# Three edits to a two-layer kernel on one core: how attention's probabilities are turned, and where four of the modulation's vectors are made

## The chip, the cores and the metric

The kernel runs on one core of a Trainium2 chip, as one launch. The metric is device time in microseconds (us), the median of several runs. A core has five engines with queues of their own: TensorE (PE in the profile; its weight loads are PEld), VectorE (DVE), ScalarE (ACT), GpSimd (POOL) and SyncE (SP), which here only issues DMAs; 16 DMA engines move the data between HBM and the core's memory SBUF. TensorE writes to PSUM.

## The reference, cut to what matters

Two layers of a diffusion transformer over 1024 rows of 1024 columns (x) and 256 rows of context (ctx). Each layer makes six vectors of 1024 from the conditioning c, the modulation:

```
m = silu(cond) @ w + b
sh1, sc1, gt1, sh2, sc2, gt2 = split(m, 6)
hx = rmsnorm(x, g) * (1 + sc1) + sh1
x = x + gt1 * mixer(hx)
x = x + gt2 * ec_moe(modulate(x, norm_ffn_g[layer], sh2, sc2))
```

So vectors 3 and 4 of a layer (sh2, sc2) are the shift and scale ahead of its experts, and vectors 2 and 5 are gates. Layer 0's mixer is a chunked mLSTM (4 heads) beside window attention (8 heads of 64, two key heads, blocks of 128 queries that see up to three blocks of keys and the 256 of the context, softmax with a sink); layer 1's is a gated MLP. `ec_moe` lets each of 16 experts take its 128 best rows by a router's softmax (top k over rows), runs silu(x Wg) * (x Wu) Wd on them with three 1024x1024 weights, and adds the result back to those rows.

## The kernel before, in words

All arithmetic is float32. A float32 product that must be exact is split: each operand into a high part (rounded to the fp32r type) and a low part, and three fp32r matmuls (high-high, low-high, high-low) stand for one. ScalarE makes the high part, VectorE the low one by a subtraction (`split`, L70 and L71). A scheduler puts the instructions of each engine into a fixed order, by the order in which the program writes them and by when it expects their inputs; tiles come from pools with a number of slots, and an instruction waits until its slot is free.

Stages, with their time in the profile:

- *Start* (0 to about 92): `start` loads ctx and x (pool "xp", ten slots of 128x1024, tag "xt"), makes layer 0's vectors 0 and 1 for x and ctx (`start_mod`), normalizes the rows and turns them. `heads_context` makes keys and values of the mLSTM's context: for each of four heads two projections, with a convolution between; between the projections it takes steps from a generator (`more`) that turns x into columns.
- *Attention and projections* (92 to 600): `layer0_a`. `attention` goes over four pairs of heads and eight blocks of 128 queries each. For a block: scores S in PSUM, their maximum (VectorE), the exponential P with its sum (ScalarE), the reciprocal of the sum. Then P (128 queries x 512 or 640 keys) is turned to keys x queries, block by block of 128x128, and split (PH, PL) for the product with the values. Before, the turn is a matmul of the block with a diagonal matrix `dg` that holds the reciprocals, so one matmul turns and divides (L480, L492). Between these parts, `fill(n)` takes steps of other work out of a generator: the projections of the next heads (L298, three 128x512 matmuls for each of eight column blocks), and now and then one step of the modulation, 9 of them for 28 steps.
- The modulation's other ten vectors come from `mod_part` (L660): for each of eight row blocks of w_mod a 128x1024 tile (0.5 MB, issued on POOL, two slots) and four matmuls that use a quarter of TensorE's columns each (L670, two passes, so eight instructions), then the bias (VectorE), and either a row written out (gates) or two transposes and a copy into `modc`.
- *mLSTM and output projection* (600 to 820), `layer0_b`; near its end each finished block of rows goes through the router (`route_tile`).
- *Routing* (820 to 862): `route` finds each expert's 128th largest score by sorting on VectorE; TensorE does little. `lists` makes row lists; `fetch` gathers an expert's rows by an indirect DMA on POOL.
- *Experts* (862 to 1430): `experts`, for each expert gate, up and down product (L1134). Weights come as 1 MB tiles (256x1024) into a ring of slots with the tag "mraw" (`moe_tile`, `moe_raw`): two slots in "gx" and eight that `layer0_b` opens near 746, five more after it: 15. Loads go on SP's queue in order, each waiting for its slot. Those whose number lies in `HELD` = (11, 14) are issued on POOL behind expert 0's row gather instead (`self.fetched`), so that they don't stand before it.
- Layer 1's gated MLP (to about 2050), its routing and experts, and the final norm, to the end. They have their own ring (`mraws` is emptied first).

Of the kernel before, what the change touches and what calls it, by code (L numbers as in the profile page):

```python
# [18 lines left out]
D = 1024  # L19
N = 1024  # L20
NT = 8
KD = 8
# [16 lines left out]
class Kernel:  # L39
# [142 lines left out]
    def start(self, rings):  # L182
        nc, I = self.nc, self.I
        with ExitStack() as late:
# [32 lines left out]
            self.heads_context(late, pt, Ws, rows())  # L217

    def heads_context(self, s, pt, Ws, more):
# [225 lines left out]
    def attention(self, hp, c, Q, fill):  # L445
# [6 lines left out]
        for n in range(NT):  # L452
# [17 lines left out]
            for i in range(2):  # L470
# [16 lines left out]
            for i in range(2):  # L487
                if i:
                    fill(self.FILLS[1])
                P, dg = Ps[i]  # L490
# [60 lines left out]
    def layer0_a(self, rings):  # L551
        nc, I = self.nc, self.I
        with ExitStack() as s:
# [60 lines left out]
            mods = itertools.chain(*(self.mod_part(lm, pa, pt, i // 6, i % 6) for i in range(2, 12)))  # L614
# [4 lines left out]
            def fill(n):  # L619

                for _ in itertools.islice(work, n):
                    i = next(steps)
                    if 9 * (i + 1) // 28 > 9 * i // 28:
                        next(mods, None)
# [35 lines left out]
    def mod_part(self, pool, pa, pt, layer, w):  # L660


        nc, I = self.nc, self.I
        acc = pa.tile([128, 512], F32, tag="acc", name="acc")[:, 0:256]
        for k in range(KD):
            wm = pool.tile([128, D], F32, tag="wm", name="wm")
            nc.gpsimd.dma_start(out=wm, in_=I["w_mod"][layer, k * 128:(k + 1) * 128, D * w:D * (w + 1)])  # L667
            lhs = self.silw[:, k].rearrange("p a s -> p (a s)")
            for j in range(4):
                nc.tensor.matmul(acc[32 * j:32 * j + 32, :], lhs, wm[:, 256 * j:256 * (j + 1)], start=(k == 0), stop=(k == KD - 1))  # L670
            yield
        rows = pool.tile([128, 256], F32, tag="mrows", name="mrows", bufs=1)
        bias = pool.tile([128, 256], F32, tag="mbias", name="mbias", bufs=1)
        b = I["b_mod"]
        nc.gpsimd.dma_start(out=bias, in_=bass.AP(tensor=b.tensor, offset=b.offset + 6 * D * layer + D * w, ap=[[256, 4], [0, 32], [1, 256]]))
# [4 lines left out]
        else:  # L680
            tr = pt.tile([128, 512], F32, tag="tr", name="tr")
            for t in range(2):
                nc.tensor.transpose(tr[:, t * 128:(t + 1) * 128], rows[:, t * 128:(t + 1) * 128], self.ident)
            nc.vector.tensor_copy(self.modc[:, layer, 8 * w:8 * w + 8].rearrange("p (j t) -> p j t", t=2),
                                  tr[:, 0:256].rearrange("p (t j r) -> p j t r", t=2, j=4)[:, :, :, 0])
        yield

# [125 lines left out]
    def layer0_b(self, l0):  # L813
# [8 lines left out]
        with ExitStack() as s:  # L822
# [43 lines left out]
            self.moe_open(self.m0, 0, 8)  # L866
            lp = self.pool(s, "lp2")
# [94 lines left out]
    def route(self, p, pp, layer):  # L962
# [10 lines left out]
        nc.tensor.transpose(tr[:, 0:128], lg.rearrange("p t e -> p (t e)"), self.ident)  # L973
# [123 lines left out]
    def moe_raw(self, name, layer, e, kp):  # L1097
        held = self.HELD[0] <= self.mrawi < self.HELD[1]
# [9 lines left out]
    HELD = (11, 14)  # L1108
# [454 lines left out]
    def run(self):  # L1563
        nc = self.nc
        with ExitStack() as es:
# [53 lines left out]
            with ExitStack() as r:  # L1619
                rw = self.pool(r, "rw0")  # L1620
                pp = self.pool(r, "rpp0", bufs=3, space=PSUM)
                self.route(rw, pp, 0)
# [78 lines left out]
```

## Time and profile before

| | |
|---|---|
| runs before | 2724.99, 2725.24, 2725.42 us; median 2725.24 |
| profiled execution | 2720.4 us; span of its instructions 2718.6 us |
| TensorE busy | 2529.9 us, 93% |
| VectorE busy | 1879.9 us, 69% |
| ScalarE busy | 1511.4 us, 56% |
| GpSimd busy | 626.0 us, 23% |
| chain that ended last, by engine | TensorE 80%, VectorE 8%, DMA 4%, issue 4%, ScalarE 3%, GpSimd 1% |
| moved by DMA | 644 MB, 237 GB/s over the span |

How to read it: the busy share is a mean over stages of different kinds, so what an edit is worth is read from its own stage. Matmuls overlap: a row's duration is longer than the distance to the next one's start. The chain of waits follows the work back from the last instruction; "issue" is time in which nothing that the profile shows was waited for. PEclk is TensorE's granted clock, 1.00 being 2.4 GHz and 0.50 being 1.2 GHz. A DMA share of 1.0 means that all 16 DMA engines moved packets all the time.

### The profile page before, as it was taken

The numbers are of one execution on the slowest core, as the hardware profiler recorded it, in microseconds if no ns is written. First come the engines' busy times: TensorE is split into PE (matmuls) and PEld (weight loads), VectorE is DVE, ScalarE is ACT, GpSimd is POOL, SyncE is SP. The second block draws the span as 40 slices with busy tenths as digits, with TensorE's granted clock in tenths as the row PEclk, the third lists the DMA queues.
The fourth block names the chain that finished last, engine by engine and source line by source line (L and its number), as shares of the span: only waits on it lengthen the run. The fifth ranks groups of instructions, "written<-read, shape, count | busy, mean of one in ns | idle before, by whom it ended". The sixth has DMA issues, their size and how long they took to land.

```text
span 2718.6 us, 35149 instructions
## 1 busy us (share of the span) xinstructions
PE 2529.9 (93%) x12847; PEld 2005.4 (74%) x12847; DVE 1879.9 (69%) x2830; ACT 1511.4 (56%) x2258; POOL 626.0 (23%) x413
## 2 busy tenths in 40 slices
PE   5999999998895999999998999999995999999996
PEld 3767777777774788888776887888884788888774
DVE  5566656567737999999885184116505899999887
ACT  4344344334424888888775223232322888888774
POOL 0010111115421222221102434533451021231001
PEclk8999999999996999999999999999997999999998
DMA  7344554457166999999966323342335999999995
GB/s 261 103 128 141 152 160 142 144 185 265 48 238 234 352 388 380 387 380 386 374 215 202 101 67 119 117 147 70 101 108 190 376 373 388 380 381 382 359 363 186
DMA packets 241642, 644.02 MB, mean 237 GB/s; under 512 B 18609, under 2 KB 85341, under 8 KB 240445
## 3 DMA queue, kind: packets, MB, share of 16 engines
q1 hardware_dynamic: 205136, 530.52, 52.3%
q0 software_dynamic: 25840, 89.99, 11.7%
q10 hardware_dynamic: 10492, 21.26, 2.3%
q8 instruction: 101, 1.65, 0.2%
q14 instruction: 73, 0.59, 0.1%
HBM read 589.06 MB, written 50.02 MB: 235 GB/s over the span
## 4 chain that ended last, share of the span: by engine, by line
PE 80%; DVE 8%; DMA 4%; issue 4%; ACT 3%; POOL 1%; POOLq 0%; ACTq 0%; SPq 0%; DVEq 0%
PE g L1134 13%; PE u L1134 13%; PE d L1134 12%; PE acc L298 8%; PE acc L1444 7%; PE acc L1518 6%; PE acc L1466 6%; PE S L492 2%; PE acc L805 2%; PE acc L670 2%; DMA wm<-in_w_mod_dram 1%; PE tr L1164 1%; DVE s2k L1460 1%; PE tr L1208 1%; PE O L501 1%
## 5 line engine op out<-in xcount | busy, mean ns | idle before, releaser
L71 DVE TENSOR_TENSOR ml<-mraw,mh 128x1024 fp32r<-128x1024 f32 x750 | 875.3, 1222 | 61.7 <-ACT mh L70 61.2
L70 ACT ACTIVATE mh<-mraw 128x1024 fp32r<-128x1024 f32 x750 | 769.3, 1064 | 138.6 <-PE g L1134 67.8
L71 POOL TENSOR_TENSOR wl<-wraw,wh 128x1024 fp32r<-128x1024 f32 (+1 forms) x132 | 253.6, 1930 | 349.8 <-ACT wh L70 349.8
L70 ACT ACTIVATE wh<-wraw 128x1024 fp32r<-128x1024 f32 (+1 forms) x163 | 143.0, 893 | 311.0 <-issue 123.6
L1232 POOL DMA_INDIRECT s_x<-xe,idx x28 | 66.9, 2388 | 655.0 <-ACT hidH L1210 394.4
L1134 PE MATMUL g<-mh,xH 128*128 128x512 f32 x512 | 206.4, 403 | 1.4 <-ACT xH L1169 1.4
L1134 PE MATMUL g<-ml,xH 128*128 128x512 f32 x512 | 205.3, 401 | 1.5 <-DVE ml L71 1.4
L1134 PE MATMUL g<-mh,xL 128*128 128x512 f32 x512 | 204.4, 399 | 0.0
L1134 PE MATMUL u<-ml,xH 128*128 128x512 f32 x512 | 203.4, 397 | 0.2
L1134 PE MATMUL u<-mh,xL 128*128 128x512 f32 x512 | 202.2, 395 | 0.0
L1134 PE MATMUL u<-mh,xH 128*128 128x512 f32 x512 | 202.2, 395 | 0.0
L1134 PE MATMUL d<-ml,hidH 128*128 128x512 f32 x496 | 197.5, 398 | 5.0 <-DVE ml L71 4.9
L1152 POOL DMA_INDIRECT xe<-s_xr,idx x32 | 137.7, 4303 | 270.7 <-ACT mh L70 131.0
L1134 PE MATMUL d<-mh,hidH 128*128 128x512 f32 x496 | 198.2, 400 | 1.6 <-DVE o L1229 1.6
L1134 PE MATMUL d<-mh,hidL 128*128 128x512 f32 x496 | 196.3, 396 | 0.0
L1444 PE MATMUL acc<-wh,h2k 128*128 128x512 f32 x512 | 163.7, 400 | 1.8 <-DVE h2k L1426 1.7
L1466 PE MATMUL acc<-h2k,wh 128*128 128x512 f32 x512 | 161.5, 396 | 0.0
L298 PE MATMUL acc<-hH,wh 128*128 128x512 f32 (+1 forms) x368 | 155.4, 422 | 1.6 <-DVE mrows L676 0.5
L1518 PE MATMUL acc<-wh,s2k 128*128 128x512 f32 x480 | 152.1, 397 | 0.0
L298 PE MATMUL acc<-hL,wh 128*128 128x512 f32 (+1 forms) x368 | 145.7, 396 | 0.0
L298 PE MATMUL acc<-hH,wl 128*128 128x512 f32 (+1 forms) x368 | 145.7, 396 | 0.0
L667 POOL DMA_DIRECT2D wm<-in_w_mod_dram x80 | 42.7, 534 | 406.6 <-PE acc L670 382.1
(469 smaller groups left out, 5238.9 us busy)
## 6 DMA issues: line engine op xcount, KB each, us to landing
mraw<-in_moe_w_down_dram SPq DMA_DIRECT2D x128, 1024.0 KB
mraw<-in_moe_w_gate_dram SPq DMA_DIRECT2D x126, 1024.0 KB
mraw<-in_moe_w_up_dram SPq DMA_DIRECT2D x124, 1024.0 KB
wm<-in_w_mod_dram POOLq DMA_DIRECT2D x80, 512.0 KB, 4.2
wraw<-in_gm_w_in_dram SPq DMA_DIRECT2D x64, 512.0 KB
wraw<-in_gm_w_out_dram SPq DMA_DIRECT2D x32, 512.0 KB
wraw<-in_ab_w_in_dram SPq DMA_DIRECT2D x30, 512.0 KB
wm<-in_w_mod_dram SPq DMA_DIRECT2D x8, 1024.0 KB
```

What stands on the lines that cost most here:

```text
L70: nc.scalar.activation(h, src, AF.Copy)
L71: i = (nc.gpsimd if eng == "pool" else nc.vector).tensor_tensor(l, src, h.bitcast(F32), op=ALU.subtract)
L298: nc.tensor.matmul(acc, a[:, k, :], b[:, k, c0:c0 + n], start=(k == 0 and i == 0), stop=(k == KD - 1 and i == 2))
L492: nc.tensor.matmul(S[i][:, 512 - nl + j * 128:640 - nl + j * 128], P[:, j * 128:(j + 1) * 128], dg, start=True, stop=True)
L670: nc.tensor.matmul(acc[32 * j:32 * j + 32, :], lhs, wm[:, 256 * j:256 * (j + 1)], start=(k == 0), stop=(k == KD - 1))
L805: nc.tensor.matmul(acc, a[:, k, t * 128:(t + 1) * 128], b[:, k % 2, :], start=(k == 0 and i == 0), stop=(k == 3 and i == 2))
L1134: nc.tensor.matmul(acc[:, sl], a[:, k, :], b[:, sl], start=(k == 0 and i == 0), stop=(k == KD - 1 and i == 2))
L1152: f = nc.gpsimd.indirect_dma_start(out=xe, out_offset=None, in_=self.s_xr[layer], in_offset=bass.IndirectOffsetOnAxis(ap=self.idx[e], axis=0))
L1232: nc.gpsimd.indirect_dma_start(out=self.s_x[layer], out_offset=bass.IndirectOffsetOnAxis(ap=self.idx[e], axis=0), in_=o, in_offset=None, c ...
L1444: nc.tensor.matmul(acc[t], a[k][:, ts], b[:, k2, :], start=(k == 0 and i == 0), stop=(k == KD - 1 and i == 2))
L1466: nc.tensor.matmul(acc, a[:, k, :], b[k], start=(k == 0 and i == 0), stop=(k == KD - 1 and i == 2))
L1518: nc.tensor.matmul(acc, a[:, ts], b[k2], start=(c == 0 and i == 0), stop=(c == 15 and i == 2))
```

## The change

1. `attention`: `dg` goes. After the first fill, VectorE multiplies P itself, in place, by the reciprocals (a value per partition), and each block is turned by a plain transpose against the identity.
2. `start` and `heads_context`: vectors 2 and 3 of layer 0 are made there. The w_mod tiles use slots of "xp", and the steps stand between the context's projections, 1, 0, 1, 2, 3, 3, 3, 3 at a time and two at the end.
3. Vectors 3 and 4 of layer 1 (`HOLE`) are made in layer 0's routing. `hole_load` takes the first eight tiles of the experts' ring for their 8 MB, on SP's queue, in `layer0_b`; `hole_mods` does the matmuls behind the routing's first transpose; ScalarE copies and GpSimd adds the bias. The expert weights then begin with the ring's ninth number, and for layer 0 the held ones are numbers 18 to 22, weights 10 to 14, in place of weights 11 to 13.
4. The fills carry the six vectors that are left, one modulation step for every five steps.

```diff
@@ start, heads_context
+            pm = self.pool(late, "pmod0", space=PSUM)
+            mods = itertools.chain(*(self.mod_part(xp, "xt", sm, pm, pt, 0, w) for w in (2, 3)))
+            self.heads_context(late, pt, Ws, rows(), mods)
...
             list(itertools.islice(more, 2))
+            list(itertools.islice(mods, (1, 1, 3, 3)[hd]))
...
             list(itertools.islice(more, 2))
+            list(itertools.islice(mods, (0, 2, 3, 3)[hd]))
         store(*kept)
-        for _ in more:
+        for _ in itertools.chain(more, mods):
@@ attention
-                dg = hp.tile([128, 128], F32, tag="dg", name="dg", bufs=2)
-                nc.vector.tensor_scalar(dg, self.ident, den, None, op0=ALU.mult)
-                Ps.append((P, dg))
+                Ps.append((P, den))
             fill(self.FILLS[0])
...
+                P, den = Ps[i]
+                nc.vector.tensor_scalar(P[:, 0:w], P[:, 0:w], den, None, op0=ALU.mult)
                 for j in range(nt):
-                    nc.tensor.matmul(S[i][:, 512 - nl + j * 128:640 - nl + j * 128], P[:, j * 128:(j + 1) * 128], dg, start=True, stop=True)
+                    nc.tensor.transpose(S[i][:, 512 - nl + j * 128:640 - nl + j * 128], P[:, j * 128:(j + 1) * 128], self.ident)
@@ layer0_a
-            mods = ... for i in range(2, 12)))
+            mods = ... for i in range(4, 12) if (i // 6, i % 6) not in self.HOLE))
...
-                    if 9 * (i + 1) // 28 > 9 * i // 28:
+                    if next(steps) % 5 == 4:
                         next(mods, None)
@@ layer0_b
             self.moe_open(self.m0, 0, 8)
+            self.hole_load()
@@ route
+        if layer == 0:
+            with self.tc.issue_after(last.ins):
+                self.hole_mods(p, self.hole_ps, self.hole_pt)
@@ moe_raw
-    HELD = (11, 14)
+    HELD = ((18, 23), (11, 14))
@@ new
+    HOLE = ((1, 3), (1, 4))
+    def hole_load(self):
+        self.hole = []
+        for layer, w in self.HOLE:
+            for kp in range(4):
+                raw = self.moe_tile()
+                self.nc.sync.dma_start(out=raw, in_=self.I["w_mod"][layer, 256 * kp:256 * (kp + 1), D * w:D * (w + 1)].rearrange("(k p) c -> p k c", p=128))
+                self.hole.append(raw)
+    def hole_mods(self, p, ps, pt):
+        for i, (layer, w) in enumerate(self.HOLE):
+            acc = ps.tile([128, 512], F32, tag="mod", name="mod")[:, 0:256]
+            for k in range(KD):
+                self.mod_step(acc, k, self.hole[4 * i + k // 2][:, k % 2, :])
+            rows = p.tile([128, 256], F32, tag="mrows", name="mrows", bufs=2)
+            self.nc.scalar.activation(rows, acc, AF.Copy)
+            self.mod_columns(rows, pt, layer, w, lambda o, x: self.nc.scalar.activation(o, x, AF.Copy))
+            m = self.modc[:, layer, 8 * w:8 * w + 8]
+            self.nc.gpsimd.tensor_tensor(m, m, self.bcols[:, 48 * layer + 8 * w:48 * layer + 8 * w + 8], op=ALU.add)
```

`mod_step` (the four matmuls), `mod_bias` and `mod_columns` (two transposes and a copy into `modc`) are `mod_part`'s old lines under names of their own.

## Rows read from the trace of the kernel before

**Rows 1.** Stretches: us, busy by engine (instructions), PEclk, DMA share, GB/s.
```profile
0.00:36.00 36.00, 13.58 (x82) 3.74 (x82) 7.94 (x38) 4.14 (x7) 1.02 (x7) 0.96 0.89 315
...
52.00:92.00 40.00, 29.06 (x212) 26.36 (x212) 37.68 (x76) 26.11 (x44) 0.34 (x2) 0.90 0.41 114
92.00:136.00 44.00, 43.49 (x217) 32.74 (x218) 17.14 (x25) 14.13 (x21) 2.01 (x3) 0.94 0.32 87
136.00:600.00 464.00, 457.24 (x2933) 346.09 (x2931) 281.40 (x613) 183.23 (x378) 53.45 (x98) 1.00 0.48 149
...
820.00:862.00 42.00, 10.64 (x59) 8.47 (x57) 30.87 (x140) 13.04 (x22) 7.07 (x10) 0.51 0.44 162
840.00:850.00 10.00, 2.64 (x9) 1.73 (x9) 6.44 (x32) 0.00 (x0) 0.00 (x0) 0.50 0.00 0
862.00:1294.00 432.00, 429.79 (x2036) 346.42 (x2036) 407.72 (x424) 364.90 (x447) 93.55 (x25) 1.00 1.01 381
```

**Rows 2.** Chain of waits, 136 to 600 us: share of the stretch by line.
```profile
by line: PE acc L298 42.2%; PE S L492 14.3%; issue 10.8%; PE acc L670 9.0%; PE O L501 4.1%; DMA wm<-in_w_mod_dram 4.1%; PE O L502 3.7%; PE S L462 1.9%; PE S L464 1.8%; PE S L463 1.8%; PE S L465 1.3%; PE S L466 1.3%; ACT P L475 1.0%; DVE ast
```

**Rows 3.** Chain of waits near the experts' end: start us, us, what, instructions.
```profile
1294.65 11.20 PE u L1134 x48
...
1313.75 5.40 PE d L1134 x22
```

**Rows 4.** TensorE's timeline in attention: start us, us, instruction, [idle before it].
```profile
335.91 1.28 PE L492 MATMUL S<-dg,P 128*128 128x128 f32 x10
336.95 0.48 PE L298 MATMUL acc<-hH,wh 128*128 128x512 f32 x1
...
340.61 0.39 PE L298 MATMUL acc<-hL,wh 128*128 128x512 f32 x1
340.83 0.40 PE L298 MATMUL acc<-hH,wl 128*128 128x512 f32 x1
341.16 0.64 PE L670 MATMUL acc<-wm,silw 128*32 128x256 f32 x8
341.73 0.50 PE L298 MATMUL acc<-hH,wh 128*128 128x512 f32 x1
```

**Rows 5.** TensorE's groups, 136 to 600: count, busy us, mean ns, idle before.
```profile
L492 PE MATMUL S<-dg,P 128*128 128x128 f32 x608 | 81.2, 280 | 2.3 <-DVE ast L477 1.7 <-DVE dg L480 0.6
```

**Rows 6.** A plain transpose in that stretch: timeline, then ns min/median/max.
```profile
585.75 0.60 PE L537 MATMUL tr<-cst,hx 128*128 128x128 f32 x4
586.10 0.48 PE L298 MATMUL acc<-hH,wh 128*128 128x512 f32 x1
...
L537 PE MATMUL tr<-cst,hx x32: 272/272/328, 252.1 to 586.1; 128*128 128x128 f32 x32
```

**Rows 7.** VectorE's groups, 136 to 600.
```profile
L314 DVE SCALAR_TENSOR_TENSOR hx<-pad,convw,hx 128x1024 f32<-128x1024 f32 x32 | 41.0, 1280 | 0.2
...
L480 DVE TENSOR_SCALAR dg<-cst,ast 128x128 f32<-128x128 f32 x64 | 18.1, 286 | 3.8 <-issue 2.3
...
L312 DVE TENSOR_SCALAR hx<-pad,convw 128x1024 f32<-128x1024 f32 x8 | 6.0, 753 | 0.0
```

**Rows 8.** SP's timeline before and in the first routing.
```profile
746.24 1.97 SPq L1105 DMA_DIRECT2D mraw<-in_moe_w_gate_dram  x4
...
787.92 0.43 SPq L1105 DMA_DIRECT2D mraw<-in_moe_w_gate_dram  x1
...
834.61 0.38 SPq L1105 DMA_DIRECT2D mraw<-in_moe_w_gate_dram  x1
854.43 0.38 SPq L1105 DMA_DIRECT2D mraw<-in_moe_w_up_dram  x1
```

**Rows 9.** POOL's timeline in the first routing.
```profile
852.83 1.31 POOL L1152 DMA_INDIRECT xe<-s_xr,idx  x1 [21.23 <-DVE gate L1071]
854.13 0.74 POOL L1103 DMA_DIRECT2D mraw<-in_moe_w_gate_dram  x1
854.88 1.39 POOL L1103 DMA_DIRECT2D mraw<-in_moe_w_up_dram  x2
```

More of the change, by code (lines that the diff above doesn't have):

```diff
@@ L215, in rows, with heads_context @@
                         yield
-            self.heads_context(late, pt, Ws, rows())
-    def heads_context(self, s, pt, Ws, more):
+            pm = self.pool(late, "pmod0", space=PSUM)
+            mods = itertools.chain(*(self.mod_part(xp, "xt", sm, pm, pt, 0, w) for w in (2, 3)))
+            self.heads_context(late, pt, Ws, rows(), mods)
+    def heads_context(self, s, pt, Ws, more, mods):
         nc = self.nc
@@ L489, in attention @@
                     fill(self.FILLS[1])
-                P, dg = Ps[i]
+                P, den = Ps[i]
+                nc.vector.tensor_scalar(P[:, 0:w], P[:, 0:w], den, None, op0=ALU.mult)
                 for j in range(nt):
-                    nc.tensor.matmul(S[i][:, 512 - nl + j * 128:640 - nl + j * 128], P[:, j * 128:(j + 1) * 128], dg, start=True, stop=True)
+                    nc.tensor.transpose(S[i][:, 512 - nl + j * 128:640 - nl + j * 128], P[:, j * 128:(j + 1) * 128], self.ident)
                 src = S[i][:, row].rearrange("p (j q) -> p j q", q=128)
@@ L613, in layer0_a @@
             Qs = [Q, [], [], []]
-            mods = itertools.chain(*(self.mod_part(lm, pa, pt, i // 6, i % 6) for i in range(2, 12)))
+            mods = itertools.chain(*(self.mod_part(lm, "wm", lm, pa, pt, i // 6, i % 6) for i in range(4, 12) if (i // 6, i % 6) not in self.HOLE))
             work = itertools.chain(*(itertools.chain(self.query(pa, qp, c + 1, hx, Qs[c + 1]) if c < 3 else (),
@@ L621, in fill @@
                 for _ in itertools.islice(work, n):
-                    i = next(steps)
-                    if 9 * (i + 1) // 28 > 9 * i // 28:
+                    if next(steps) % 5 == 4:
                         next(mods, None)
@@ L657, in key_stack, with mod_step, mod_bias @@
                                         kh[base:base + 64, c0:c0 + n].bitcast(F32), op=ALU.subtract)
-    def mod_part(self, pool, pa, pt, layer, w):
-        nc, I = self.nc, self.I
+    def mod_step(self, acc, k, wm):
+        for j in range(4):
+            self.nc.tensor.matmul(acc[32 * j:32 * j + 32, :], self.silw[:, k].rearrange("p a s -> p (a s)"), wm[:, 256 * j:256 * (j + 1)],
+                                  start=(k == 0), stop=(k == KD - 1))
+    def mod_bias(self, pool, layer, w, bufs=1):
+        b = self.I["b_mod"]
+        bias = pool.tile([128, 256], F32, tag="mbias", name="mbias", bufs=bufs)
+        self.nc.gpsimd.dma_start(out=bias, in_=bass.AP(tensor=b.tensor, offset=b.offset + 6 * D * layer + D * w, ap=[[256, 4], [0, 32], [1, 256]]))
+        return bias
@@ new lines, in mod_columns, with mod_part @@
+    def mod_columns(self, rows, pt, layer, w, copy):
+        tr = pt.tile([128, 512], F32, tag="tr", name="tr")
+        for t in range(2):
+            self.nc.tensor.transpose(tr[:, t * 128:(t + 1) * 128], rows[:, t * 128:(t + 1) * 128], self.ident)
+        copy(self.modc[:, layer, 8 * w:8 * w + 8].rearrange("p (j t) -> p j t", t=2),
+             tr[:, 0:256].rearrange("p (t j r) -> p j t r", t=2, j=4)[:, :, :, 0])
+    def mod_part(self, wp, tag, pool, pa, pt, layer, w):
+        nc = self.nc
@@ L664, in mod_part @@
         acc = pa.tile([128, 512], F32, tag="acc", name="acc")[:, 0:256]
         for k in range(KD):
[L666 to L670, printed above, removed]
+            wm = wp.tile([128, D], F32, tag=tag, name="wm")
@@ L671, in mod_part @@
+            nc.gpsimd.dma_start(out=wm, in_=self.I["w_mod"][layer, k * 128:(k + 1) * 128, D * w:D * (w + 1)])
+            self.mod_step(acc, k, wm)
             yield
+        bias = self.mod_bias(pool, layer, w)
         rows = pool.tile([128, 256], F32, tag="mrows", name="mrows", bufs=1)
-        bias = pool.tile([128, 256], F32, tag="mbias", name="mbias", bufs=1)
-        b = I["b_mod"]
-        nc.gpsimd.dma_start(out=bias, in_=bass.AP(tensor=b.tensor, offset=b.offset + 6 * D * layer + D * w, ap=[[256, 4], [0, 32], [1, 256]]))
@@ L680, in mod_part @@
         else:
[L681 to L685, printed above, removed]
-        yield
+            self.mod_columns(rows, pt, layer, w, nc.vector.tensor_copy)
+        yield
+    HOLE = ((1, 3), (1, 4))
[16 more added lines that the diff above has]
+            self.nc.gpsimd.tensor_tensor(m, m, self.bcols[:, 48 * layer + 8 * w:48 * layer + 8 * w + 8], op=ALU.add)
     def lstm_main(self, lp, hd):
@@ L972, in route @@
         tr = pp.tile([128, 512], F32, tag="tr", name="tr")
-        nc.tensor.transpose(tr[:, 0:128], lg.rearrange("p t e -> p (t e)"), self.ident)
+        last = nc.tensor.transpose(tr[:, 0:128], lg.rearrange("p t e -> p (t e)"), self.ident)
         rows = p.tile([128, 128], F32, tag="rows", name="rows")
@@ L1097, in moe_raw @@
     def moe_raw(self, name, layer, e, kp):
-        held = self.HELD[0] <= self.mrawi < self.HELD[1]
+        h0, h1 = self.HELD[layer]
+        held = h0 <= self.mrawi < h1
         raw = self.moe_tile()
@@ L1621, in run @@
                 pp = self.pool(r, "rpp0", bufs=3, space=PSUM)
+                self.hole_ps = self.pool(r, "rmod", bufs=2, space=PSUM)
+                self.hole_pt = self.pool(r, "rmpt", bufs=2, space=PSUM)
                 self.route(rw, pp, 0)
```

## The prediction, made before the changed kernel was built

> **What bounds the kernel now.** I read the busy table by stretches first [rows 1]. The stretches are the ones that the edits touch: the start (0 to 136 us), layer 0's attention with its projections (136 to 600), the first routing (820 to 862) and layer 0's experts (862 to 1430). In the attention stretch TensorE is busy 457 of 464 us at clock 1.00, VectorE 281, the DMA engines 48%: TensorE's own work sets the time there. Then the chain of waits of that stretch [rows 2]: 42.2% projections (L298), 14.3% the matmuls that turn P (L492), 9.0% the modulation matmuls (L670). From 52 to 92 VectorE is the full one (37.7 of 40 us; TensorE 29.1), from 92 to 136 TensorE again (43.5 of 44). In the routing TensorE works 10.6 of 42 us at clock 0.51, and from 840 to 850 the DMA engines move nothing at all. In the experts TensorE (430 of 432 us) and the DMA engines (share 1.01, 381 GB/s) are both full; near the end the DMA side loses: an up group that began at 1294.65 lasts 11.20 us, and the down group behind it doesn't start before 1313.75 [rows 3], TensorE's first break of that kind.
>
> So a microsecond of TensorE work taken out of 136 to 600 is worth a microsecond, if nothing late takes its place; TensorE work put into the routing is free; and a megabyte that the experts start without has to be paid back at 381 GB/s.
>
> **The change part by part.**
>
> *Plain transposes.* A block of 128x128 of P costs two passes today: ten L492 instructions (five blocks) start at 335.91 and the next matmul starts at 336.95, so 1.04 us, 0.208 us a block [rows 4]. There are 608 such instructions [rows 5], 304 blocks: 304 x 0.208 = 63 us; the chain's 14.3% of 464 us = 66 us agrees. A plain transpose of the same shape stands in the same stretch: four L537 start at 585.75, the next matmul at 586.10, 0.35 us, 0.09 us each [rows 6]. 304 x 0.09 = 27 us. Saved: 36 us of TensorE. What bounds it: nothing (the P operand could make it no cheaper) to 39 us (the chain's 66 less 27). I take 36, because the row has the same shape, type and engine state.
>
> The row of the transposes says 0.60 us for four, and one of them alone lasts 0.27 [rows 6]; their starts, not their durations, are what the next matmul waits for. The Trainium skill ("TensorE: Matmul & The Clock Gate", Part 4: PE-mode transpose) gives about 275 ns for a transpose within a kernel. The trace agrees with that as a duration and not as a price per transpose; paid in full it would make the edit a loss (a rival below).
>
> *VectorE's side of it.* The diagonal (128x128, 0.286 us, 64 times) goes; P itself is scaled, 128x640 (48 times) or 128x512 (16). No row has this shape; between 0.286 us at 128 columns and 0.753 at 1024 [rows 7] a straight line gives 0.55 and 0.49. That is 48 x 0.55 + 16 x 0.49 - 64 x 0.286 = +16 us on VectorE: from 281 of 464 to 297 of about 411, 72%. It doesn't become the bound by its sum. But the scaling is 0.26 us longer than what it replaces, and it is issued after the four fill steps, behind what these put into VectorE's queue (convolution steps of 1.28 us). Queued behind it on TensorE are the five transposes, and behind these everything that TensorE has in order. Today TensorE loses almost nothing here: its idle time in front of L492 is 2.3 us in the whole stretch [rows 5], since other steps are put in front while P isn't ready. With 58 us less of such steps some waits will show. Bounds: 0, and 64 x 0.9 = 58 us (0.26 plus half of a 1.28 us step, each time in full). I take 5 us, near the low end, because the row of today is near zero and VectorE keeps over a quarter of its time free.
>
> *Modulation steps that leave the stretch.* A step is eight L670 instructions: the L298 before it starts at 340.83, the one behind it at 341.73, 0.90 us; an ordinary L298 gap is 0.22 (340.61 to 340.83) [rows 4], so a step costs 0.67 us. Four of the ten parts leave (two to the start, two to the routing): 32 steps x 0.67 = 21 us, and six of twelve small transposes, 0.5 us. Saved: 22 us. The fills then hold 54 modulation steps where there were 90. Their 16 MB of DMA also leave, where the engines are half idle: worth nothing.
>
> Attention stretch: -36 - 22 + 5 = -53 us.
>
> *Two parts between the context projections.* 16 steps x 0.67 = 11 us come to TensorE between 40 and 100. The cover is the 52 to 92 stretch: TensorE has 11 us free there, VectorE none; on VectorE only two short additions and a small copy come in. What isn't done at 92 is paid in full, as TensorE is the bound from there to 136. Also 8 MB move there, at 41% DMA share, free, except for the first two tiles: they reuse the context's rows, which are free while the start still waits for its own weights at share 0.89 (315 GB/s over 0 to 36) [rows 1]; 1.05 MB at 381 GB/s is 2.8 us, and what shares the engines is late by up to that. Bounds: -2 (a TensorE that idles less may have its faster clock: it is 0.90 in that stretch) to 11 + 2.8 = 14 us. I take +4: most of the 2.8 and a step or two behind 92.
>
> *Two parts in the first routing.* TensorE's 16 steps (11 us, up to 21 at half clock) lie between the first transpose and the sort's end; it has 31 free us. Four ScalarE copies and two small GpSimd additions come with them, and the fetch of expert 0's rows (852.83 on POOL) stands behind the additions; if the copies are held up by a conversion that waits for its weights, the fetch slips. 0 to 3 us; I take 1.
>
> *Eight tiles of the experts' ring.* The w_mod tiles take the first eight load slots of the quiet stretch, where the weights are loaded today (from 746 on). Today's count at 854.4, when the stream of weights starts again: four at 746.24 and four of the same kind behind them, one at 787.92 and one more of its kind before the routing, one at 834.61, so 11 tiles; the next three are held on POOL until the fetch, and SP's next one goes at 854.43 [rows 8, 9]. After: two tiles by 834.6 (the two of 787.92's kind). Then SP can go on at once, as five slots open at 834.61 and the modulation frees three more in time, one about each 1.4 us (two steps). From 834.6 to 854.4 at 1.05 MB / 381 GB/s = 2.75 us a tile, less 1.5 us until the first one flows: 6.6 tiles. 11 - 8.6 = 2.4 tiles x 2.75 = 6.6 us that the experts' stream ends later. Since TensorE breaks off for want of weights before the experts end, it comes out in full. Bounds: 0 (TensorE still ends last) to (11 - 2) x 2.75 = 25 us (the ring stays empty until the fetch). I take +6.5. Layer 1's experts have their own ring and don't change.
>
> *Sum*: -53 + 4 + 1 + 6.5 = -41.5 us. Made against the profiled execution (2720.4 us; span 2718.6) this is 2679; the median of the runs is 4.8 us above that execution, so 2683.
>
> **The rivals.**
>
> 1. *VectorE's queue makes the transposes late.* For: the scaling now stands behind the fills' convolution steps, and a chunk of 1.28 us [rows 7] can be in front of it. Against: the 2.3 us of today. If each of the 32 block rows loses 0.26 + 0.64 = 0.9 us once: 29 us, total -58 + 29 + 11.5 = -17.5: 2708. Chance 9%.
>
> 2. *The same, in series, and the kernel is slower.* Place: the wait of the transposes for the scaled P, in both heads of a block row, with nothing left to put in front. Price: 64 x (1.28 + 0.26) = 99 us, total -58 + 99 + 11.5 = +52: 2777. It decides from a mean of (58 - 11.5) / 64 = 0.73 us of lateness per head on. For: the fills shrink by 4 in 10 of their modulation steps. Against: the same chain has such chunks in it today, and TensorE idles 7 of 464 us. Chance 5%.
>
> 3. *A transpose costs its duration.* 304 x (0.27 - 0.208) = +19 instead of -36: 19 - 22 + 5 + 11.5 = +13.5: 2739. Against: 0.35 us for four [rows 6]. Chance 2%. The figure of the Trainium skill (above) would come to this.
>
> 4. *The ring stays empty until the fetch* (slots held by late modulation steps): +25 instead of +6.5: 2702. Against: TensorE has three times the time that it needs. Chance 5%.
>
> 5. *All of it hidden* (no new waits, start and ring free): -58: 2667. For: TensorE idles little in any of these. Chance 8%.
>
> 6. *The transposes as dear as today*, so that the change doesn't do what it says: 36 us less gain, -5.5: 2720. Chance 3%.
>
> **How the numbers follow.** The forecast has 68%, and its own range is 2668 to 2698: waits of 0 to 12, start 0 to 8, ring 3 to 10. The time is 2683. The range 2662 to 2712 takes in rivals 1, 4 and 5; left out are rivals 2, 3, 6 and the tails. A difference of over 0.2% (5.5 us) is what a measurement of this kernel can tell from none. Faster by that: 68 + 9 + 5 + 8 in 100, 0.90; within: rival 6, 0.03; slower: rivals 2 and 3, 0.07.
>
> **What would show it.** The L492 line is gone and transposes start 0.09 us apart; the stretch from 136 lasts about 411 us instead of 464, TensorE still over 96% busy; a tensor_scalar on P of 0.55 us. In the start, modulation matmuls between 50 and 95, and the first TensorE work of the projections at most 3 us later. In the routing, TensorE busy in the first half, no empty 840 to 850 on the DMA side, the fetch within 3 us of its place. In the experts, the first break of TensorE some experts earlier (the lead is 2.4 tiles smaller) and the end of the weights about 6 us later, counted from the fetch. Wrong would be: the attention stretch above 430 us with TensorE waiting for VectorE, or experts longer by over 12 us.

## The result, and the profile after

The changed kernel takes 2695.79 us (median of 3 runs, 2693.89 to 2698.45), against 2725.24 before: a ratio of 0.9893, 95% interval 0.9870 to 0.9915, so 29.5 us faster. The forecast was 2683, 42 us faster, with 2668 to 2698 as its own range. The profiled execution took 2693.89 us (span 2692.1), 26.5 less than that of before; by stages, between instructions that both kernels have:

| from ... to | before | after | difference | forecast |
|---|---|---|---|---|
| begin, first matmul of scores | 156.3 | 173.0 | +16.7 | +4 |
| ... last product with the values | 427.5 | 373.3 | -54.2 | -53 |
| ... last router matmul | 240.8 | 237.9 | -2.9 | 0 |
| ... gather of expert 0's rows issued | 28.2 | 36.3 | +8.1 | +1 |
| ... first expert matmul | 8.6 | 8.8 | +0.2 | 0 |
| ... end of layer 0's experts | 580.2 | 583.4 | +3.1 | +6.5 |
| ... first expert matmul of layer 1 | 669.1 | 672.1 | +3.0 | 0 |
| ... end | 607.8 | 607.3 | -0.5 | 0 |

The stretches of the kernel after, in the columns of [rows 1]:

```profile
52.00:92.00 40.00, 35.15 (x262) 26.23 (x263) 33.15 (x72) 22.80 (x40) 8.38 (x15) 0.91 0.75 237
...
153.00:546.00 393.00, 381.76 (x2278) 289.73 (x2277) 286.59 (x594) 179.75 (x373) 32.00 (x56) 1.00 0.39 122
786.00:832.00 46.00, 18.75 (x174) 11.01 (x175) 29.50 (x130) 14.30 (x24) 8.81 (x12) 0.61 0.81 305
832.00:1410.00 578.00, 569.86 (x2653) 456.05 (x2653) 532.60 (x547) 471.50 (x578) 95.39 (x32) 1.00 0.95 355
```

In the attention TensorE is still busy 97% of the time. Between the context's projections, from 52 to 92 us, it isn't: 35.2 of 40 us, with the DMA engines at 0.75 (0.41 before) and VectorE less busy than before (33.2 us against 37.7), though nothing was taken from it.

*Attention.* Groups of 153 to 546 us after, as in [rows 5] and [rows 7], TensorE's and then VectorE's:

```profile
L495 PE MATMUL S<-cst,P 128*128 128x128 f32 x304 | 43.8, 276 | 3.0 <-DVE ast L481 1.7 <-DVE P L493 1.1
L665 PE MATMUL acc<-wm,silw 128*32 128x256 f32 x384 | 38.4, 390 | 3.2 <-DMA wm<-in_w_mod_dram 3.2
...
L493 DVE TENSOR_SCALAR P<-P,ast 128x640 f32<-128x640 f32 x48 | 26.2, 553 | 1.0
```

Of the 3.2 us that TensorE waits for w_mod in this window, 2.3 lie ahead of the first scores (at 173.0). From there to the last product the wait is 0.9 us, the same as before (us in total, times, longest):

```profile
PE acc L665 <- DMA wm<-in_w_mod_dram: 0.9, 2, 0.5
```

TensorE's timeline, as [rows 4]; five blocks take 0.47 us to the next matmul where they took 1.04:

```profile
333.22 0.71 PE L495 MATMUL S<-cst,P 128*128 128x128 f32 x5
333.69 0.47 PE L302 MATMUL acc<-hH,wl 128*128 128x512 f32 x1
```

Summed from start to next start over the whole attention, the turning of P costs 33.8 us where it cost 66.7: 0.11 us a block. The row's 276 ns agrees with the Trainium skill's 275 ns ("TensorE: Matmul & The Clock Gate", Part 4: PE-mode transpose) as a duration, though the page measured bfloat16 and P is float32; the price was less than half of it.

*Start.* The waits for the projections' own weights in the chain of waits from 56 to 110 us, first before, then after:

```profile
77.53 3.77 DMA wraw<-in_ab_w_in_dram
```

```profile
61.08 6.00 DMA wraw<-in_ab_w_in_dram
...
75.34 8.96 DMA wraw<-in_ab_w_in_dram
...
89.33 8.97 DMA wraw<-in_ab_w_in_dram
...
100.67 3.04 DMA wraw<-in_ab_w_in_dram
```

That is 27.0 us where it was 3.8, for loads that the change doesn't touch (the first three of 0.5 MB each). What stands beside them is in POOL's timeline (six w_mod tiles issued in a row):

```profile
67.78 3.12 POOL L688 DMA_DIRECT2D wm<-in_w_mod_dram  x6 [8.99 <-PE acc L665]
73.65 0.53 POOL L688 DMA_DIRECT2D wm<-in_w_mod_dram  x1 [2.74 <-PE acc L665]
```

*Routing.* Timeline of all engines after; in brackets the idle time before and who ended it:

```profile
787.85 9.28 PE L665 MATMUL mod<-mraw,silw 128*32 128x256 f32 x128
...
788.29 0.23 DVE L1014 COPY work<-rows 128x128 f32<-128x128 f32 x1
...
797.21 0.35 DVE L1030 MAX8 sort<-work 128x8 f32<-128x64 f32 x2 [8.69 <-PE mod L665]
...
797.32 0.52 POOL L1022 TENSOR_TENSOR res<-lg,aux 128x128 f32<-128x128 f32 x1 [9.10 <-PE mod L665]
```

The sort has its input at 788.52 and starts at 797.21, with the modulation's last matmul. It doesn't use what that matmul makes.

*Experts.* SP's loads, as [rows 8], then POOL's, as [rows 9]:

```profile
748.08 0.43 SPq L1146 DMA_DIRECT2D mraw<-in_moe_w_gate_dram  x1
...
753.98 0.41 SPq L1146 DMA_DIRECT2D mraw<-in_moe_w_gate_dram  x1
...
791.11 0.67 SPq L1146 DMA_DIRECT2D mraw<-in_moe_w_up_dram  x1
794.68 0.90 SPq L1146 DMA_DIRECT2D mraw<-in_moe_w_gate_dram  x2
795.63 1.55 SPq L1146 DMA_DIRECT2D mraw<-in_moe_w_up_dram  x3
797.23 4.02 SPq L1146 DMA_DIRECT2D mraw<-in_moe_w_gate_dram  x2
```

```profile
820.48 1.87 POOL L1193 DMA_INDIRECT xe<-s_xr,idx  x1 [20.41 <-DVE gate L1111]
822.77 1.45 POOL L1144 DMA_DIRECT2D mraw<-in_moe_w_gate_dram  x2 [0.42 <-issue]
```

Ten weights are on their way by 801, eight of them only since the modulation began to free their slots.

The prediction read [rows 3] as TensorE's first break for want of weights. It isn't one: TensorE is busy there all the time, and the down group begins at 1306.48 and not at 1313.75. What [rows 3] shows is where the chain of waits leaves TensorE for the engines that prepare its next operands. Kernel before, a stretch in the columns of [rows 1], and TensorE's timeline:

```profile
1305.85:1313.75 7.90, 7.83 (x43) 6.20 (x41) 6.13 (x8) 7.43 (x14) 0.00 (x0) 1.00 0.88 324
```

```profile
1306.48 0.48 PE L1134 MATMUL d<-mh,hidH 128*128 128x512 f32 x1
```

How much TensorE lacks weights is better read from its waits for their low part (`ml`, VectorE's last step on a weight), summed over layer 0's experts: us in total, times, longest, before and then after, 2.6 us and 3.9 us:

```profile
PE d L1134 <- DVE ml L71: 2.0, 2, 1.0
PE g L1134 <- DVE ml L71: 0.6, 1, 0.6
```

```profile
PE d L1175 <- DVE ml L71: 2.9, 3, 1.0
PE g L1175 <- DVE ml L71: 1.0, 2, 0.6
```

### The profile page after: what moved, and what is told of

It reads as the page before. It is cut to its first block, busy times and chain, and to the rows that moved or that the text cites. A ratio compares the mean times of both kernels' runs of the same rounds, so it can differ in the third digit from the quotient of the medians.

```text
span 2692.1 us, 34493 instructions
## 1 busy us (share of the span) xinstructions
PE 2495.9 (93%) x12543; PEld 1972.3 (73%) x12543; DVE 1891.8 (70%) x2826; ACT 1508.6 (56%) x2262; POOL 610.6 (23%) x399
## 4 chain that ended last, share of the span: by engine, by line
PE 78%; DVE 9%; issue 4%; DMA 4%; ACT 3%; POOL 1%; POOLq 0%; ACTq 0%; DVEq 0%; SPq 0%
PE g L1175 13%; PE u L1175 13%; PE d L1175 12%; PE acc L302 7%; PE acc L1485 7%; PE acc L1559 6%; PE acc L1507 6%; PE acc L841 2%; PE S L495 1%; DMA wm<-in_w_mod_dram 1%; DMA wraw<-in_ab_w_in_dram 1%; PE acc L665 1%; PE tr L1205 1%; PE tr L1249 1%; DVE s2k L1501 1%
## 5 line engine op out<-in xcount | busy, mean ns | idle before, releaser
L1193 POOL DMA_INDIRECT xe<-s_xr,idx x32 | 148.3, 4634 | 256.4 <-ACT mh L70 125.7
L1273 POOL DMA_INDIRECT s_x<-xe,idx x28 | 45.1, 1612 | 683.0 <-ACT hidH L1251 446.8
L688 POOL DMA_DIRECT2D wm<-in_w_mod_dram x64 | 34.6, 543 | 442.3 <-PE acc L665 388.9
```

Source lines behind the costliest of these rows:

```text
L688: nc.gpsimd.dma_start(out=wm, in_=self.I["w_mod"][layer, k * 128:(k + 1) * 128, D * w:D * (w + 1)])
L1193: f = nc.gpsimd.indirect_dma_start(out=xe, out_offset=None, in_=self.s_xr[layer], in_offset=bass.IndirectOffsetOnAxis(ap=self.idx[e], axis=0))
L1273: nc.gpsimd.indirect_dma_start(out=self.s_x[layer], out_offset=bass.IndirectOffsetOnAxis(ap=self.idx[e], axis=0), in_=o, in_offset=None, c ...
```

## The experiments

Times are medians beside runs of the kernel before on the same chip (2723.7 to 2724.9). In short:

| run | us | ratio, 95% interval |
|---|---|---|
| e1, plain transposes alone | 2713.65 | 0.9952 (0.9934 to 0.9969) |
| e2, two vectors back from the start | 2708.90 | 0.9938 (0.9919 to 0.9956) |
| e3, start loads one tile per vector | 2689.22 | 0.9869 (0.9848 to 0.9889) |
| e4, pool kept | 2692.60 | 0.9885 (0.9864 to 0.9906) |
| e5, e1 with half tiles | 2702.37 | 0.9918 (0.9900 to 0.9936) |
| e6, e4 with half tiles | 2687.04 | 0.9859 (0.9841 to 0.9877) |
| e7, no vector in the routing | 2705.97 | 0.9934 (0.9909 to 0.9958) |
| e8, e6 with one queue | 2670.66 | 0.9799 (0.9781 to 0.9817) |
| e9, one queue alone | 2681.05 | 0.9833 (0.9817 to 0.9850) |
| e10, the changed kernel again | 2697.11 | 0.9890 (0.9874 to 0.9907) |
| e11, e8 with a third vector | 2690.95 | 0.9879 (0.9858 to 0.9899) |
| e12, e8 with nothing held | 2685.96 | 0.9865 (0.9849 to 0.9882) |

### The transposes: e1 and e5

e1 is the kernel before with the edit of `attention` alone.

> The kernel before with the first edit alone: P is scaled by VectorE and turned by plain transposes; all ten modulation vectors stay in the attention's fills, the start and the routing are untouched. Theory (a turned block costs TensorE about 0.1 us less, and the scaling is hidden): -30 to -35 us against before, so about 2692; start and routing as before (first score matmul at 156 us, last router matmul to expert 0's row gather 28 us). Rival A (most of the attention's -54 us came from the modulation steps that left, the transposes being worth 10 us or less): 2715 or more. Rival B (VectorE's scaling stands in TensorE's way once all ten vectors' additions are back in its queue): TensorE idles over 15 us in front of the transposes, 2705 or more.

Measured: 2713.65, 11 us less than before, near rival A's 2715 but not by its way. The transposes themselves cost 35.4 us instead of 66.7, much as in the whole change, but the attention only went from 427.5 to 411.1: 15 us of the 31 are lost again. Of rival B's place nothing is seen (2.7 us of idle time in front of the transposes). About half of the 15 is in what TensorE waited for (us in total, times, longest; before, then e1):

```profile
PE acc L670 <- DMA wm<-in_w_mod_dram: 0.9, 3, 0.4
```

```profile
PE acc L669 <- DMA wm<-in_w_mod_dram: 10.0, 11, 2.4
```

Of the 10.0 us, 8.8 lie behind the first scores. The other 7 of the 15 us aren't split here. The modulation's tiles have two slots and land 4.2 us after their issue. With shorter work between the steps, that would be too slow. e5 tests this:

```diff
-            wm = pool.tile([128, D], F32, tag="wm", name="wm")
+            for c in range(2):
+                wm.append(pool.tile([128, 512], F32, tag="wm", name="wm", bufs=5))
...
```

> The kernel of e1 (before with the plain transposes alone) with the fills' w_mod tile in two halves of 128x512 and five slots instead of two slots of 128x1024, so that loads are issued earlier. Theory (with the transposes, the modulation steps follow each other faster than two slots can load, 4.2 us from issue to landing, and TensorE waits 10.0 us for w_mod in e1 where it waited 0.9 before): these waits fall under 3 us, the attention from first scores to last product goes from 411 to about 403 us, the time from 2713.7 to about 2705. Rival (the tiles are late because POOL issues them late or because the DMA engines are slower, not for want of slots): waits of 8 us or more stay, 2711 to 2716.

Measured: attention 403.0, 2702.37. The time is as expected, but only in part for the expected reason: the waits fell by 2.9 us, from 8.8 to 5.9, which lies between theory and rival, and the attention by 8.1. The want of slots is shown for these 2.9 us; where the rest came from is not.

```profile
PE acc L671 <- DMA wm<-in_w_mod_dram: 5.9, 7, 1.4
```

### The start: e2, e3, e9 and e10

e2 undoes the second edit:

```diff
-            mods = itertools.chain(*(self.mod_part(xp, "xt", sm, pm, pt, 0, w) for w in (2, 3)))
+            mods = itertools.chain(*(self.mod_part(xp, "xt", sm, pm, pt, 0, w) for w in ()))
...
-            mods = ... for i in range(4, 12) if ...
+            mods = ... for i in range(2, 12) if ...
...
```

> The changed kernel with layer 0's vectors 2 and 3 made in the attention's fills again (13 modulation steps for 50), nothing else undone. Theory (moving them to the start cost 16.7 us there and gave back 16 steps of 0.67 us = 11 us in the attention): first score matmul back at about 156 us instead of 173, attention 11 us longer, so about 6 us faster than the changed kernel: 2690. Rival (the start is late for another reason than these two vectors, such as the order that the scheduler chose): first score matmul stays above 168 us and the kernel is 5 to 11 us slower than the changed one: 2701 to 2707.

Measured: 2708.90, slower than the changed kernel. The start half of the theory held: first scores at 157.1. The attention half didn't: 398.2 us, not 11 but 25 us longer. 16 steps at 0.67 are 11; 9 more are waits for w_mod (10.2 us where the changed kernel has 0.9 between the same points); the rest, 5, I can't split.

```profile
PE acc L666 <- DMA wm<-in_w_mod_dram: 10.2, 5, 2.4
```

So the vectors were right to leave, and the loss in the start had to be looked for there. e3 takes its loads away:

```diff
-            wm = wp.tile([128, D], F32, tag=tag, name="wm")
-            nc.gpsimd.dma_start(...)
+            if tag == "wm" or k == 0:
+                wm = wp.tile([128, D], F32, tag=tag, name="wm")
+                nc.gpsimd.dma_start(...)
```

> The changed kernel, but in the start each of the two vectors loads one w_mod tile instead of eight and uses it for all its eight steps (the two vectors come out of the wrong weights); all 16 steps of matmuls, the bias and the columns stay where they are: 7 MB of DMA left out. Theory (the start lost its time to the loads: the projections' weights land up to 9 us after their issue instead of 4, and TensorE's steps wait for their own tiles): first score matmul at 158 to 163 us instead of 173, total 2683 to 2687. Rival (the time went into the steps themselves, in series with the projections on TensorE, and into VectorE's queue): 169 us or later, total above 2691.

Measured: first scores at 165.2, 2689.22, between the two. 7.8 of the 16.7 us went with the loads, and 9 stayed, up to 3 of them from the two early tiles (first projection at 43.1 instead of 40.2). The chain's waits for the projections' weights fell from 27.0 to 10.1 us:

```profile
62.62 5.36 DMA wraw<-in_ab_w_in_dram
...
81.29 4.73 DMA wraw<-in_ab_w_in_dram
```

e9 keeps all loads and all steps, and changes the queue that issues them:

```diff
-            nc.gpsimd.dma_start(out=wm, in_=self.I["w_mod"][...])
+            (nc.sync if tag == "xt" else nc.gpsimd).dma_start(out=wm, in_=self.I["w_mod"][...])
```

> The changed kernel with one word changed: the start's w_mod tiles are issued on SP's queue instead of POOL's (no kept pool, no half tiles). Theory (e8's start came from the order of the loads alone): first score matmul at 157 to 160 us instead of 173, w_in tiles no longer in the chain of the start, routing as in the changed kernel (36 us from last router matmul to row gather), time 2695.8 - 15 = 2680, 2677 to 2684. Rival (e8 was faster because its three edits work together): first score matmul above 165 us, or 2688 and more.

Measured: 2681.05, first scores at 158.3: 14.7 of the 16.7 us are gone. SP's timeline in e9 shows the projections' weights between the modulation's tiles, and the stretch (columns of [rows 1]) TensorE at 37.6 of 40 us and 281 GB/s, where the changed kernel has 35.2 us and 237 GB/s:

```profile
65.23 2.37 SPq L688 DMA_DIRECT2D wm<-in_w_mod_dram  x5
69.33 0.38 SPq L78 DMA_DIRECT2D wraw<-in_ab_w_in_dram  x1
69.80 3.57 SPq L688 DMA_DIRECT2D wm<-in_w_mod_dram  x3
73.47 0.39 SPq L78 DMA_DIRECT2D wraw<-in_ab_w_in_dram  x1
```

```profile
52.00:92.00 40.00, 37.58 (x329) 28.57 (x332) 37.54 (x78) 25.10 (x43) 1.58 (x4) 1.00 0.86 281
```

No wait for these weights is left in e9's chain. So it is not these megabytes by themselves that cost the time but that they came through a second queue. Two things changed along with the queue and aren't taken apart: the scheduler gave TensorE another order of work, and TensorE's granted clock from 52 to 92 us is 1.00 where the changed kernel and e3 have 0.91. Why e3, with hardly any loads, is later than e9 with all of them stays open: its order of work differs too, and it still waits 10.1 us for the projections' weights although the DMA engines are at 0.38 there.

e10 is the changed kernel once more.

> The changed kernel itself, unchanged, beside e9 and the kernel before on one chip. Theory: 2693 to 2698 again, first score matmul at 173 us, gather 36 us after the last router matmul; layer 1 from the end of layer 0's experts to its own first expert matmul 671 to 673 us, as in all experiments so far, even those that leave the ring alone, so that the 3 us above the one profile of before are not the change's. Rival (the 3 us are the change's, by the rows that layer 1 loads late): 669 us would be seen in no run with the ring's edit and stay a mark of kernels without it.

Measured: 2697.11, first scores at 171.7, gather after 36.6 us. Layer 1's stretch was 670.9 us; it was 672.7, 671.2 and 672.8 in e1, e5 and e7, which have the ring of before. And e12, which has the ring's edit, has 669.9. So the 3.0 us aren't the ring's; whether they are any edit's can't be said from one profile of before.

### The routing and the ring: e4, e7 and e12

e4 keeps the pool of `silw`, the modulation's stationary operand, until the routing is over:

```diff
-                mc = self.pool(l0, "mcol")
+                mcs = es.enter_context(ExitStack())
+                mc = self.pool(mcs, "mcol")
...
                 self.route(rw, pp, 0)
+            mcs.close()
```

> The changed kernel, with the pool that holds the lhs of the modulation's matmuls (silw) kept until the end of the first routing, so that the routing's tiles lie elsewhere in SBUF and need not wait until the modulation's last matmul has read it. Theory (the sort's first MAX8 waits 8.7 us for the last modulation matmul because its output tile lies on silw): MAX8 starts about 0.3 us after the copy of the scores, last router matmul to expert 0's row gather 28 to 30 us instead of 36, total about 2688. Rival (VectorE and GpSimd are held by another tie to TensorE, such as its order of matmuls or the small matmuls of the sort that stand behind the modulation): still 34 us or more, total 2695.

Measured: gather after 28.7 us, so the theory holds; VectorE's timeline in e4:

```profile
791.33 0.23 DVE L1014 COPY work<-rows 128x128 f32<-128x128 f32 x1
791.59 0.35 DVE L1030 MAX8 sort<-work 128x8 f32<-128x64 f32 x2
```

But of these 7.6 us the kernel got about 3 (2692.60; the intervals of the two kernels overlap): the experts took 587.5 us instead of 583.4. One thing that changed is in POOL's timeline, the second gather now stands in front of the held weights, which went out 2.3 us behind the first gather in the changed kernel:

```profile
815.88 1.32 POOL L1193 DMA_INDIRECT xe<-s_xr,idx  x1 [13.72 <-DMA mraw<-in_moe_w_gate_dram]
828.37 1.22 POOL L1193 DMA_INDIRECT xe<-s_xr,idx  x1 [11.17 <-DVE oh L1098]
829.57 0.80 POOL L1144 DMA_DIRECT2D mraw<-in_moe_w_gate_dram  x1
```

That this is the reason isn't shown. TensorE's waits for the weights' low part grew by 1.0 us only (4.9 instead of 3.9); for the same 2670 matmuls it was busy 579.0 us instead of 575.6, at a mean granted clock of 0.99 instead of 1.00.

e7 undoes the third edit:

```diff
-    HOLE = ((1, 3), (1, 4))
-    HELD = ((18, 23), (11, 14))
+    HOLE = ()
+    HELD = ((11, 14), (11, 14))
```

> The changed kernel with the two vectors of the routing made in the attention's fills again (13 steps for 50, half tiles as in e5), so no w_mod tile in the experts' ring; the start is as changed. Theory (the routing's part costs 8 us in the routing and 3 to 4 us in the experts' weights, and saves 16 steps of 0.67 us = 11 us in the attention, so that it is worth nothing): last router matmul to row gather 28 us, experts' end 617 to 620 us after the last router matmul instead of 628, attention 384 us instead of 373, time within 4 us of the changed kernel, 2692 to 2699. Rival (two vectors more in the fills cost 25 us, as the step from the changed kernel to e2 seems to say, whatever the slots): attention 395 us or more, 2705 or more.

Measured: 2705.97. Routing and ring are as expected: gather after 28.2 us, experts' end 619.9 after the last router matmul (628.5 in the changed kernel), TensorE's waits for the weights' low part 2.6 us, as before. But the attention takes 389.9 us where e6, with the same half tiles, takes 371.1: two vectors cost 19 us there, not 11. So the vectors in the routing are worth about 10 us net (2705.97 against 2695.79; the ends of the intervals overlap), with all that they cost.

e12 sends the held weights on SP's queue too (`HELD = ((18, 18), (11, 14))`, on top of e8).

> The kernel of e8 with no expert weight held back on POOL behind expert 0's row gather in layer 0: all loads go on SP's queue as their slots come free. In e8 the five held loads go out 12 to 19 us after that gather's issue, since the second gather stands ahead of them on POOL. Theory (the experts of layer 0 are long by what their weights come late: 585.3 us in e8, 582.3 to 583.6 in kernels without w_mod in the ring): the loads go out before the gather, experts 582 to 584 us, time 2667 to 2669. Rival (loads in front of the gather make it land late, which the holding prevents): gather 8 to 20 us instead of 5.8 us from issue to landing, the first expert matmul as much later, time 2672 to 2685.

Measured: 2685.96, 15 us slower than e8; the theory fell. The gather landed after 7.9 us, close to the rival's 8, and the first expert matmul came 2.1 us later behind it, but 12 us are in the experts (597.6 us): TensorE's waits for the weights' low part are 9.6 us instead of 4.9, and it was busy 6.8 us longer. At a full DMA share the weights came in more slowly, first e8, then e12:

```profile
900.00:1000.00 100.00, 100.00 (x476) 80.89 (x475) 95.78 (x99) 85.63 (x107) 17.99 (x6) 1.00 1.03 396
```

```profile
900.00:1000.00 100.00, 100.00 (x473) 80.77 (x472) 95.76 (x97) 84.62 (x101) 24.97 (x6) 1.00 1.02 382
```

Why is open.

### Together: e6, e8 and e11

e6 is e4 with e5's half tiles, e8 adds e9's queue.

> The changed kernel with e4's kept pool and e5's half tiles in the fills. Theory (3.2 us of waits for w_mod left in the changed kernel's attention, gone with more slots): attention 370 us instead of 373, time about 2690 against e4's 2692.6. Rival (these waits are covered elsewhere): as e4.

Measured: 2687.04, attention 371.1 (372.7 in e4). The profiled execution was no shorter than e4's (span 2692.7 against 2691.7), so this is a small gain at most, and not by the theory: the wait for w_mod between the first scores and the last product is 2.0 us in e6 and 0.2 in e4. The 3.2 us of the theory counted a wait ahead of the first scores.

> The kernel of e6 with the start's w_mod tiles issued on SP's queue, in one order with the projections' weights and behind the rows of x, instead of on POOL. Theory (the start lost 2.9 us to two tiles that were loaded ahead of the start's own weights, and part of 7.8 us to bursts of up to seven tiles in front of the projections' weights): first context projection back at 40 to 41 us, first score matmul at 163 to 167 us instead of 173, time 2680 to 2684. Rival (the order in one queue makes the projections' weights wait for the modulation's slots): first score matmul at 172 us or later, 2689 or more.

Measured: 2670.66, better than both kernels: 54 us under before. First context projection at 41.6, first scores at 158.2, earlier than expected: as in e9, one queue gave back nearly all.

> The kernel of e8 with a third vector (layer 0's vector 5, a gate) made in the start, between the same projections, and one modulation step for every six steps in the fills. Theory (the start's DMA share of 0.86 and TensorE's 9 free us leave no room for 4 MB and 5.4 us more, while the attention gives back 8 steps of 0.7 to 1.0 us): first score matmul 5 to 8 us later than e8's 158, attention 6 to 8 us shorter, time within 3 us of e8's 2670.7. Rival A (the start still has room): first score matmul at 160 us or earlier, 2662 to 2666. Rival B (the loads get in front of the projections' weights again): 170 us or later, 2677 or more.

Measured: 2690.95. First scores at 171.5, as in rival B, and the attention gave back 6.4 us (365.3). The chain waits for more than the projections' weights, though:

```profile
65.78 6.37 DMA wm<-in_w_mod_dram
...
80.00 7.74 DMA wraw<-in_ab_w_in_dram
...
95.98 6.44 DMA s_ckv<-ckv
```

From 56 to 110 us the DMA engines are at 0.95, where e9 has 0.82: so with a third vector the bytes seem to count in one queue too, which no run takes apart from the order of work. Ten more us lie in layer 1 before its experts (681.5 us); I have no cause for them.

## Why the prediction was right and wrong

*The time.* 2695.79 lies 13 us above the forecast (whose sum makes 2683.7), near the upper end of its own range. Start and routing both fell outside the bounds that I had given them; that the total stayed inside is in part luck, since two errors in the attention cancelled and the ring cost less than I took.

*What bounds the kernel: right.* TensorE is still the bound of the attention (97% busy), and what the whole change took from it there came out of the time.

*Plain transposes: right.* -36 forecast, -32.9 measured (0.11 us a block, not 0.09); the scaling of P took 0.553 us (0.55). The new waits that I put on VectorE, forecast at 5 us, are 0.7 us (3.0 instead of 2.3 in front of the transposes).

*The sum of the attention: right, but the two terms aren't independent, as I had them.* Counted from start to next start, the turning of P gives -32.9, the matmuls of modulation and projections together -22.4 (forecast -22), and the rest +1.1: -54.2. Done alone, the transposes give -16.4 (e1), and the four vectors that leave afterwards 37.8 (411.1 to 373.3). The prediction looked for what is late next on VectorE; about half of what e1 loses is a wait for the modulation's own tiles, hidden at the old pace with 0.9 us and not at the new one (8.8 us). With 32 steps fewer that wait is back at 0.9.

*Two parts between the context projections: wrong, the mis-sized term.* +4 forecast, bounds -2 to 14; +16.7. The step that failed is "Also 8 MB move there, at 41% DMA share, free, except for the first two tiles". The first two tiles cost what I said (first projection at 43.3 instead of 40.2; 42.0 in e10). The others came in bursts on POOL's queue as slots of "xp" came free, and the path waited 6 to 9 us for each of three loads of the projections' weights on SP's queue, which it needed first. I asked how many bytes the engines could take over 40 us, and not what is in front of a load that the path waits for. In one queue the same work costs 2.0 us (e9), half of what I forecast.

*Two parts in the first routing: wrong.* 1 forecast, bounds 0 to 3; 8.1. I counted each engine's free time and the queues, and these were right: TensorE did the 16 steps in 9.3 us. What I didn't look at is where the routing's tiles lie: on `silw`, whose pool was closed while the moved step still reads it, so the sort had to wait for the last reader. e4 gives 7.6 us of it back.

*Eight tiles of the ring: right in sign, too large.* +6.5 forecast; the experts' stage is 3.1 us longer, with a routing 8 us longer in which weights could still load, but TensorE's waits for weights grew by 1.3 us only (2.6 to 3.9). The step that failed is "Since TensorE breaks off for want of weights before the experts end, it comes out in full": the break that I had read from [rows 3] isn't one, and TensorE was busy 7.83 of 7.90 us there. The length of the stage alone doesn't tell the ring's cost: e1, e5 and e7, without w_mod in the ring, have the 2.6 us of waits that before has, and still take 582.3 to 583.6 us where before takes 580.2. In these three TensorE's clock falls to its lower level (1.2 GHz) for some 3 us, 30 us after the first expert matmul (granted clock 0.52 from 872.0 to 875.5 us of e7); in before and in the changed kernel it doesn't, though TensorE was as busy in the 12 us ahead of that point (9.8 us in e7, 9.9 in the other two), and why is open. With the routing mended (e4, e6, e8, e11) the waits are 4.9 us. So by TensorE's waits the ring costs 1.3 us in the changed kernel and 2.3 with the routing mended.

## What to carry to other kernels

A free share of the DMA engines doesn't make a load free: ask which load the path waits for next and what will stand before it, and put moved loads into the queue of those that they could delay, as long as the engines have room for the bytes (e9 had it; e11, with one vector more, seems not to). When a step is moved, look for the memory that it still reads as well as for engines and queues; a closed pool is a wait without any dependence of data. And an edit that makes a stretch shorter brings its loads nearer: a wait that was hidden at the old pace can take back a part of the gain (8 of 31 us in e1), so edits measured one by one need not add up. Last, where the chain of waits leaves an engine, look at that engine's own timeline before you call it a break.

## What the runs showed of the hardware

While POOL's queue held a burst of tiles, SP's queue got as many packets from the DMA engines as POOL's, and so far fewer bytes. From 77 to 80 us of the changed kernel (packets, MB, share of 16 engines; q0 is POOL's, q1 SP's; SP's two loads of the projections' weights were issued at 72.93 and 75.34):

```profile
q0 software_dynamic: 289, 1.05, 88.4%
q1 hardware_dynamic: 282, 0.14, 16.1%
```

POOL's packets are 3.6 KB here and SP's 0.5 KB, and POOL's w_mod got seven times the bytes of the weights that the path waited for, which came in at 48 GB/s. From 81 to 83 us, when POOL's queue moved nothing, they came in at 294 GB/s:

```profile
q1 hardware_dynamic: 1165, 0.59, 121.8%
```

The Trainium skill ("DMA: Bandwidth & Descriptors", Queues, rings and completion order) says that a DMA engine takes turns between queues packet by packet. The equal counts agree with it (289 and 282; in e10, from 75 to 78 us, 288 and 286): the queue with the smaller packets gets fewer bytes for its turns. No run varied the size of the packets, and from 95 to 98 us, behind the bursts, the counts are 143 and 867.
